# Last expert's tail, last chunk's products, slot lists and turned rows rearranged in a hybrid layer with expert-choice MoE

## Chip, core and metric

The kernel is one program on one core of one Trainium2 chip. The metric is the device time of an execution in microseconds (us). Engines are named as in the profile: PE (TensorE matmul), PEld (its weight load), DVE (VectorE), ACT (ScalarE), POOL (GpSimd), SP (the queue that issues most DMAs).

## What is computed

One layer over 1024 tokens of width 1024, 256 context tokens, then a last RMSNorm. The first half (norm, projection, three mixers, merge) is not touched by the change. What follows it is:

```python
h2 = modulate(x, norm2_g, sh2, sc2)
x = x + g2 * expert_choice_ffn(h2, w_router, w_gate, w_up, w_down)
return rmsnorm(x, final_norm_g)

def expert_choice_ffn(...):            # 16 experts, each takes its 128 best tokens
    gates, idx = lax.top_k(affinity.T, cap)
    xg = h[idx]
    a, u = xg @ w_gate[e], xg @ w_up[e]            # 1024 -> 2816
    y = (silu(a) * u) @ w_down[e] * gates          # 2816 -> 1024
    return zeros.at[idx].add(y)
```

All data is fp32. A product is made of three matmuls on values split into a high part that TensorE takes at full speed (fp32r) and the rest.

## The kernel before

`moe` streams the weights of the 16 experts through the core. An expert's 2816 hidden columns are cut into six **chunks** (0 to 5): five of 512 columns and a last one of 256. A weight piece is loaded in two **halves**, and a half is the unit of everything: `halves` lists them in the order of the products, for each expert chunk by chunk gate (2 halves), up (2), down of the chunk before (2), and after the last chunk its own down (2). That makes 36 halves for an expert, 576 in all; the halves of the last chunk hold 128x1024 elements, all others 128x2048.

- `load(j)` issues the DMA of half j from SP into a ring of twelve 1 MB tiles (`RING`). SP takes its DMAs in order, so one that waits holds up all behind it.
- `split(j)` makes the two parts of half j in one of four `whl` buffers: ACT copies the high part (line 67), DVE subtracts it for the rest (line 68).
- `products(j)` runs the matmuls through `mm3` (lines 72 to 74): 12 pairs of gate or up for a half, into PSUM tiles `w_gate` and `w_up`, or `y` for down.
- `silu` (ACT, line 1203) and `gated` (DVE, line 1206) make the chunk's activations, `turn` (line 1212) transposes them on PE two halves later, and line 67/68 split them into `aT` for the down products.
- The next expert's tokens are prepared inside the current one, at chunk 2: `choose_hot` makes a one-hot matrix (DVE, line 1099), `choose_rows` multiplies it with `tv` (eight matmuls, line 1109) which gives the token numbers and gates, and POOL gathers the rows (line 1114). At chunk 4 `turned` transposes the rows on PE (line 1134), for the first half of the columns before the second gate half, for the other before the second up half, and applies the modulation: ACT writes the high part (line 1138) and again the fp32 value (line 1142), DVE subtracts (line 1143).
- `scaled` (DVE, line 1222) and `scatter` (POOL, line 1226) add an expert's result to the DRAM tensor `xacc`, six halves into the next expert.

PE, ACT and DVE are under a manual schedule there: they run in the order in which the Python code emits them. The loop emits for half j what stands in `before[j]`, its products, then `split(j + 4)` and `load(j + 15)`, then what stands in `after[j]`. So a late instruction on DVE or ACT holds up what is behind it there. Ahead of that stage (and for POOL and SP in it) a scheduler places instructions by their dependencies.

`final` runs when the last expert has ended: it loads all of `xacc` (line 1319), adds the last expert's rows by matmuls with a one-hot matrix (lines 1335, 1337), squares and sums each of eight 128-row tiles (ACT, line 1339), makes the reciprocal root (`rstd`), scales (DVE line 1349, or ACT and POOL) and stores eight tiles from SP (line 1350).

## Time and profile before

| what | us |
|---|---|
| median of three runs | 2874.66 (2870.95 to 2875.48) |
| the profiled execution | 2874.45, its span 2872.7 |
| first product of the expert stage starts | 1310.67 |
| last product of the last expert starts | 2841.33 |
| PE, DVE, ACT busy in 100 us of the stage (1800 to 1900) | 99.60, 89.89, 77.65 |

The span is what the profile covers; 1.75 us of the profiled execution lie outside it. The busy time of PE is that of pipelined matmuls: a busy PE is not PE at its peak. An engine's share is an average over the stage; what a change is worth is read from what the next instruction waits for.

### The profile page before, as it was taken

The page shows a single profiled execution, that of the slowest core. Times are in us where ns is not written, and L with a number is a line of the kernel's source. Part 1 is how long each engine was busy: PE and PEld are TensorE (multiplying, and loading weights), DVE is VectorE, ACT ScalarE, POOL GpSimd, SP SyncE. Part 2 cuts the span into 40 slices and gives each one's busy share as a digit, 9 for nine tenths or more (in the row PEclk, how much of TensorE's full clock was granted, in tenths as well). Part 3 has the DMA queues.
Part 4 walks back from the last instruction along what each step waited for, and adds up shares of the span by engine and source line. Part 5 has one row for each costly group of instructions (what it writes and reads, how often), then busy time and mean ns, then how long its engine had stood idle before and what let it go on. Part 6 is the DMA issues. An engine that isn't in the chain of part 4 may idle for free.

```text
span 2872.7 us, 36082 instructions
## 1 busy us (share of the span) xinstructions
PE 2773.3 (97%) x13607; PEld 2299.9 (80%) x13607; DVE 2036.5 (71%) x2412; ACT 1685.7 (59%) x2005; POOL 290.2 (10%) x452
## 2 busy tenths in 40 slices
PE   7999999999999989987999999999999999999997
PEld 3888888888788878866888888888888888888885
DVE  4423231234578873478889988998899889988998
ACT  5412121212068981345777777777777777777775
POOL 1111000000144420000000000000000000000000
PEclk9999999999999999998999999999999999999998
DMA  8433231224977847558999999999999999999995
GB/s 251 176 125 143 81 136 55 78 98 137 298 202 216 208 161 252 163 169 308 340 369 378 375 376 369 379 376 372 369 381 379 370 369 380 379 373 366 375 381 197
DMA packets 344303, 783.54 MB, mean 273 GB/s; under 512 B 17288, under 2 KB 61008, under 8 KB 344000
## 3 DMA queue, kind: packets, MB, share of 16 engines
q1 hardware_dynamic: 321920, 705.09, 69.5%
q0 software_dynamic: 21968, 75.99, 7.7%
q8 instruction: 107, 1.75, 0.2%
q14 instruction: 68, 0.56, 0.1%
q10 hardware_dynamic: 240, 0.16, 0.0%
HBM read 710.37 MB, written 70.80 MB: 272 GB/s over the span
## 4 chain that ended last, share of the span: by engine, by line
PE 46%; ACT 3%; DMA 2%; DVE 2%; issue 1%; DVEq 0%
PE y L74 5%; PE y L72 5%; PE y L73 5%; PE w_gate L74 5%; PE w_gate L72 5%; PE w_gate L73 5%; PE w_up L72 5%; PE w_up L74 5%; PE w_up L73 5%; DMA wraw<-in_w_up 2%; PE tp L1212 2%; ACT whl L67 1%; DVE whl L68 1%; ACT xT L1138 1%; ACT a L1142 1%
## 5 line engine op out<-in xcount | busy, mean ns | idle before, releaser
L68 DVE TENSOR_TENSOR whl<-wraw,whl 128x2048 fp32r<-128x2048 f32 (+1 forms) x656 | 1292.2, 1996 | 211.9 <-ACT whl L67 209.6
L67 ACT CAST whl<-wraw 128x2048 fp32r<-128x2048 f32 (+1 forms) x660 | 1091.2, 1671 | 413.7 <-PE y L74 125.0
L73 PE MATMUL mm<-hT,whl 128*128 128x512 f32 x768 | 301.1, 392 | 1.6 <-DVE hT L278 1.6
L72 PE MATMUL mm<-hT,whl 128*128 128x512 f32 x768 | 300.4, 392 | 1.5 <-ACT hT L272 1.5
L74 PE MATMUL mm<-hT,whl 128*128 128x512 f32 x768 | 301.0, 392 | 0.0
L74 PE MATMUL w_gate<-whl,xT 128*128 128x512 f32 (+1 forms) x768 | 286.9, 374 | 2.8 <-DVE xT L1143 2.8
L72 PE MATMUL w_gate<-whl,xT 128*128 128x512 f32 (+1 forms) x768 | 289.6, 377 | 0.0
L72 PE MATMUL w_up<-whl,xT 128*128 128x512 f32 (+1 forms) x768 | 288.3, 375 | 0.0
L73 PE MATMUL w_gate<-whl,xT 128*128 128x512 f32 (+1 forms) x768 | 286.4, 373 | 0.0
L74 PE MATMUL w_up<-whl,xT 128*128 128x512 f32 (+1 forms) x768 | 285.8, 372 | 0.0
L73 PE MATMUL w_up<-whl,xT 128*128 128x512 f32 (+1 forms) x768 | 285.4, 372 | 0.0
L72 PE MATMUL y<-whl,aT 128*128 128x512 f32 x704 | 282.0, 401 | 0.0
L74 PE MATMUL y<-whl,aT 128*128 128x512 f32 x704 | 275.3, 391 | 0.0
L73 PE MATMUL y<-whl,aT 128*128 128x512 f32 x704 | 274.9, 391 | 0.0
L72 PEld LDWEIGHTS mm<-hT,whl 128*128 128x128 f32 x768 | 144.9, 189 | 37.5 <-ACT sg L534 5.2
L73 PEld LDWEIGHTS mm<-hT,whl 128*128 128x128 f32 x768 | 145.5, 189 | 31.9 <-DVE hT L278 2.0
L74 PEld LDWEIGHTS mm<-hT,whl 128*128 128x128 f32 x768 | 145.3, 189 | 29.9
L74 PEld LDWEIGHTS w_gate<-whl,xT 128*128 128x128 f32 x768 | 145.3, 189 | 29.2 <-DVE xT L1143 3.5
L73 PEld LDWEIGHTS w_gate<-whl,xT 128*128 128x128 f32 x768 | 145.5, 189 | 25.0
L74 PEld LDWEIGHTS w_up<-whl,xT 128*128 128x128 f32 x768 | 144.7, 188 | 25.6
L72 PEld LDWEIGHTS w_gate<-whl,xT 128*128 128x128 f32 x768 | 145.4, 189 | 24.7
L1226 POOL DMA_INDIRECT xacc<-yo,tok x15 | 50.5, 3364 | 1132.7 <-DVE yo L1222 1132.7
(355 smaller groups left out, 4423.3 us busy)
## 6 DMA issues: line engine op xcount, KB each, us to landing
wraw<-in_w_gate SPq DMA_DIRECT2D x160, 1024.0 KB, 11.1
wraw<-in_w_up SPq DMA_DIRECT2D x160, 1024.0 KB, 8.8
wraw<-in_w_down SPq DMA_DIRECT2D x160, 1024.0 KB, 11.8
wraw<-in_w_in SPq DMA_DIRECT2D x28, 1024.0 KB, 5.5
wraw<-in_ada_w SPq DMA_DIRECT2D x24, 1024.0 KB, 6.8
wraw<-in_w_gate SPq DMA_DIRECT2D x32, 512.0 KB, 12.0
wraw<-in_w_up SPq DMA_DIRECT2D x32, 512.0 KB, 9.3
wraw<-in_w_down SPq DMA_DIRECT2D x32, 512.0 KB, 5.9
```

The costliest lines, as they stand in the source:

```text
L67: self.nc.scalar.copy(hi, src)
L68: (eng or self.nc.vector).tensor_sub(lo, src, f(hi))
L72: mm(out, lh, rh, start=start, stop=False, **kw)
L73: mm(out, lh, rl, start=False, stop=False, **kw)
L74: mm(out, ll, rh, start=False, stop=stop, **kw)
L1138: nc.scalar.activation(ex.xT[:, 0, kk], tp[:, cs], AF.Identity, bias=B, scale=A)
L1142: nc.scalar.activation(h32[:, cs], tp[:, cs], AF.Identity, bias=B, scale=A)
L1212: nc.tensor.transpose(tp[:, 128 * k:128 * k + 128], ex.ready[:, 128 * k:128 * k + 128], self.ident)
L1226: nc.gpsimd.indirect_dma_start(out=self.xacc[:, :], out_offset=bass.IndirectOffsetOnAxis(ap=ex.tok, axis=0), in_=ex.yo, in_offset=None, co ...
```

## The change

1. **Final norm beside the last expert.** `final` is gone. In the last expert's loop, five tiles of the ring are taken out for good: one for the final gain and a scratch, four for `xacc` (1 MB each). The table `late` gives the half, counted from the end (H = 544), at which each step is emitted: the rows that the last expert adds to are gathered (H-29), eight squares on ACT (H-22 to H-12), two `rstd` (H-18, H-5), eight scalings on DVE with their stores from SP (H-14 to H-3). After the loop the last expert's 128 rows are finished apart: `scaled`, plus the gathered rows, square, `rstd`, scale, and one indirect store over the rows of `out`. In the last two halves the products of the first 512 columns of `y` all come before those of the others.
2. **Last chunk's gate and up in one product.** A half of kind `both` holds 256 columns of gate and 256 of up (two DMAs of 512 KB), and a product of 512 columns takes the place of two of 256. An expert has 34 halves. `silu` and `gated` of that chunk both follow its second half.
3. **Lists turned later.** `choose_list` multiplies the other way round (the one-hot matrix moves, `tv` is the weight) into 4x128, DVE copies that, and three halves later `choose_rows` transposes it on PE and goes on as before.
4. **Rows turned in fp32 first.** `turned` writes the fp32 values by ACT, then one ACT copy and one DVE subtraction of 512 columns. Its second half is emitted six halves after chunk 4's first gate half (ahead of the first `both` half), no longer three.
5. A Silu on ACT is written ahead of the first loads, and the ring's twelve tiles come from pools of 3, 1, 5 and 3 (before: 3, 5, 1, 3).

```diff
-    def rstd(self, ss, pool, tag):
+    def rstd(self, ss, pool, tag, eps=None):
...
+        if eps is not None:
+            nc.scalar.activation(s, ss, AF.Sqrt, scale=1.0 / D, bias=eps)
         nc.vector.tensor_scalar(v, ss, 1.0 / D, EPS, op0=ALU.mult, op1=ALU.add)
-        nc.scalar.sqrt(s, v)
+        if eps is None:
+            nc.scalar.sqrt(s, v)
...
-            ring_pool("wraw3", 5)
-            ring_pool("wraw4", NR - 8 - 3)
+            ring_pool("wraw3", 1)
+            ring_pool("wraw4", NR - 7)
...
+            def choose_list(ex):
...
-                    nc.tensor.matmul(tp[:, :4], hot[:, c], self.tv[:, c, e], start=c == 0, stop=c == CB - 1)
+                    nc.tensor.matmul(tp[:4, :128], self.tv[:, c, e], hot[:, c], start=c == 0, stop=c == CB - 1)
+                ex.list = sp.tile([4, 128], F32, name="list", bufs=1)
+                nc.vector.tensor_copy(ex.list, tp[:4, :128])
+
+            def choose_rows(ex, held=None):
+
+                tp = pst.tile([128, 512], F32, name="tp")
+                nc.tensor.transpose(tp[:, :4], ex.list, self.ident[:4, :4])
...
-                    nc.scalar.activation(ex.xT[:, 0, kk], tp[:, cs], AF.Identity, bias=B, scale=A)
...
-                nc.vector.tensor_sub(ex.xT[:, 1, 4 * b:4 * b + 4], h32.rearrange("p (k t) -> p k t", t=128),
-                                     f(ex.xT[:, 0, 4 * b:4 * b + 4]))
+                    nc.scalar.activation(h32[:, cs], tp[:, cs], AF.Identity,
+                                         bias=shift[:, kk:kk + 1], scale=scale[:, kk:kk + 1])
+                ks = slice(4 * b, 4 * b + 4)
+                self.split(ex.xT[:, 0, ks], ex.xT[:, 1, ks], h32.rearrange("p (k t) -> p k t", t=128))
...
-                    todo = [("w_gate", c), ("w_up", c)] + [("w_down", c - 1)] * (c > 0) + [("w_down", c)] * (c == last)
+                    todo = [("both", c)] if c == last else [("w_gate", c), ("w_up", c)]
+                    todo += [("w_down", c - 1)] * (c > 0) + [("w_down", c)] * (c == last)
...
+            def finish_load(i):
+                t = fin[i] = ring_tile(keep=True)
+                if i == 0:
+                    g = io["final_norm_g"]
+                    nc.sync.dma_start(t[:, :D], bass.AP(tensor=g.tensor, offset=g.offset, ap=[[0, 128], [1, D]]))
+                else:
+                    nc.sync.dma_start(t.rearrange("p (s d) -> p s d", s=2),
+                                      self.xacc[256 * (i - 1):256 * i].rearrange("(s p) d -> p s d", s=2))
...
+            def finish_square(i):
...
+                nc.scalar.activation(fin[0][:, D:], fin_row(i), AF.Square,
+                                     accum_out=fin["ss", i // 4][:, i % 4:i % 4 + 1])
...
+            def finish_store(i):
+                x = fin_row(i)
+                nc.vector.scalar_tensor_tensor(x, x, fin["r", i // 4][:, i % 4:i % 4 + 1], fin[0][:, :D],
+                                               op0=ALU.mult, op1=ALU.mult)
+                nc.sync.dma_start(io["out"][128 * i:128 * i + 128], x)
...
+            late = {H - 29: [lambda ex: finish_rows(ex)]}
+            for i, lag in enumerate((22, 21, 20, 19, 17, 15, 14, 12)):
+                late.setdefault(H - lag, []).append(lambda ex, i=i: finish_square(i))
+            late.setdefault(H - 18, []).append(lambda ex: finish_rstd(0))
+            late.setdefault(H - 5, []).append(lambda ex: finish_rstd(1))
+            for i, lag in enumerate((14, 12, 8, 7, 4, 4, 3, 3)):
+                late.setdefault(H - lag, []).append(lambda ex, i=i: finish_store(i))
+
+            def stream(j):
+
+                if j < FIN:
+                    load(j)
+                elif j < FIN + 5:
+                    finish_load(j - FIN)
+                else:
+                    load(j - 5)
...
+                if j == H - 2:
+                    return
+                if j == H - 1:
+
+                    for b in range(2):
+                        bs = slice(512 * b, 512 * b + 512)
+                        for kk in range(n // 128):
...
+            nc.scalar.activation(self.cs[:, 0, 0:1], self.ident[:, 0:1], AF.Silu)
             AHEAD = 4
...
+                if s == 1 and w == "both":
+                    silu(ex, ex.h[w][:, :n])
+                    gated(ex, ex.h[w][:, n:2 * n])
+
+                    put(after, j + 1, ("first", lambda ex=ex, c=c, n=n: turn(ex, c, n)))
...
-                        put(before, j + 3, lambda nx=nxt: choose_rows(nx))
+                        put(before, j + 3, lambda nx=nxt: choose_list(nx))
+                        put(before, j + 6, lambda nx=nxt: choose_rows(nx))
                     if c == 4:
                         put(before, j + 1, lambda nx=nxt: turned(nx, 0))
-                        put(before, j + 3, lambda nx=nxt: turned(nx, 1))
+                        put(before, j + 6, lambda nx=nxt: turned(nx, 1))
...
-            for b in range(2):
-                scaled(ex, b)
-            order.close()
-            rawst.close()
-            self.final(psg, ex.yo, ex.gate)
-
-    def final(self, psg, y, gate):
...
+            ss = sp.tile([128, 4], F32, name="ss")
             for b in range(2):
                 cs = slice(512 * b, 512 * b + 512)
+                scaled(ex, b)
+                nc.vector.tensor_add(ex.yo[:, cs], ex.yo[:, cs], ex.xg[:, cs])
+                nc.scalar.activation(fin[0][:, D:][:, cs], ex.yo[:, cs], AF.Square, accum_out=ss[:, b:b + 1])
+            nc.vector.tensor_add(ss[:, 2:3], ss[:, 0:1], ss[:, 1:2])
+            r = self.rstd(ss[:, 2:3], sp, "rl", fin["eps"])
+            nc.vector.scalar_tensor_tensor(ex.yo, ex.yo, r, fin[0][:, :D], op0=ALU.mult, op1=ALU.mult)
+
+            nc.gpsimd.indirect_dma_start(
+                out=io["out"][:, :], out_offset=bass.IndirectOffsetOnAxis(ap=ex.tok, axis=0),
+                in_=ex.yo, in_offset=None)
```

How the order on the engines moves is told at three places. The first is DVE at chunk 4 of an expert that has a next one (`xT` are the next expert's rows, `a` the gated activations, `aT` their split, `whl` the weights), before:

```order
L68 TENSOR_TENSOR whl<-wraw,whl 128x2048 x2
L1143 TENSOR_TENSOR xT<-a,xT 128x512
L68 TENSOR_TENSOR whl<-wraw,whl 128x2048
L68 TENSOR_TENSOR whl<-wraw,whl 128x1024
L1143 TENSOR_TENSOR xT<-a,xT 128x512
L1206 TENSOR_TENSOR a<-a,w_up 128x512
L68 TENSOR_TENSOR whl<-wraw,whl 128x1024 x2
L68 TENSOR_TENSOR aT<-tp,aT 128x512
```

and after:

```order
L68 TENSOR_TENSOR xT<-a,xT 128x512
L68 TENSOR_TENSOR whl<-wraw,whl 128x2048 x2
L1289 TENSOR_TENSOR a<-a,w_up 128x512
L68 TENSOR_TENSOR whl<-wraw,whl 128x2048 x2
L68 TENSOR_TENSOR aT<-tp,aT 128x512
L68 TENSOR_TENSOR whl<-wraw,whl 128x2048
L68 TENSOR_TENSOR xT<-a,xT 128x512
L68 TENSOR_TENSOR whl<-wraw,whl 128x1024
L1289 TENSOR_TENSOR a<-a,w_gate 128x256
```

The second `xT` stood right ahead of chunk 4's gated product and now stands behind that chunk's `aT`.

The second is DVE at the very end, after (`rfr` is the result of `rstd` for row tiles 4 to 7, `rl` belongs to that of the last expert's rows, `wraw` is a tile of rows of `xacc`):

```order
L1191 SCALAR_TENSOR_TENSOR wraw<-wraw,rfr 128x1024 x4
L1305 SCALAR_TENSOR_TENSOR yo<-y_21647,gate,g2b 128x512
L1390 TENSOR_TENSOR yo<-yo,xg 128x512
L1305 SCALAR_TENSOR_TENSOR yo<-y_21648,gate,g2b 128x512
L1390 TENSOR_TENSOR yo<-yo,xg 128x512
L1392 TENSOR_TENSOR ss<-ss 128x1
L112 TENSOR_SCALAR rlv<-ss 128x1
L115 RECIPROCAL rlr<-rls 128x1
L116 TENSOR_TENSOR rls<-rlr 128x1
L117 TENSOR_TENSOR rls<-rls,rlv 128x1
L118 TENSOR_SCALAR rls<-rls 128x1
L119 TENSOR_TENSOR rlr<-rlr,rls 128x1
```

Four scalings of 1024 columns stand ahead of the last expert's own result; before, 16 additions and the eight tiles' norms stood behind it. The last scaling (line 1394) and POOL's store follow.

The third is ACT in the gate projection of the first half of the program, long before the experts (`sg` a sigmoid), before:

```order
L534 ACTIVATE sg<-mm 128x512 x16
L599 ACT_TABLE_LOAD
L599 ACTIVATE ss<-ident 128x1
```

and after:

```order
L537 ACTIVATE sg<-mm 128x512 x12
L1324 ACT_TABLE_LOAD
L1324 ACTIVATE cs<-ident 128x1
L537 ACT_TABLE_LOAD
L537 ACTIVATE sg<-mm 128x512 x4
L602 ACT_TABLE_LOAD
L602 ACTIVATE ss<-ident 128x1
```

The Silu that is written at the head of the expert stage (line 1324) was placed there by the scheduler, between sigmoids; a table load ahead of the first expert's Silu is still in ACT's order (`L1285 ACT_TABLE_LOAD`).

## Rows read from the trace of the kernel before

**Rows 1.** Windows: us, then busy PE, PEld, DVE, ACT, POOL (count), PEclk, DMA, GB/s

```profile
1800.00:1900.00 100.00, 99.60 (x480) 83.00 (x479) 89.89 (x60) 77.65 (x67) 4.17 (x2) 1.00 1.02 374
```

**Rows 2.** Timeline, PE, chunks 4 and 5: start, us, instruction [idle before <-releaser]

```profile
1869.35 0.39 PE L72 MATMUL y<-whl,aT 128*128 128x512 f32 x1
...
1871.84 0.39 PE L74 MATMUL y<-whl,aT 128*128 128x512 f32 x1
1872.63 0.63 PE L1212 MATMUL tp<-ident,a 128*128 128x128 f32 x4 [0.40 <-DVE a L1206]
...
1875.86 0.28 PE L72 MATMUL w_gate<-whl,xT 128*128 128x256 f32 x1
...
1881.61 0.40 PE L72 MATMUL y<-whl,aT 128*128 128x512 f32 x1
```

**Rows 3.** Timeline of ACT and DVE around the same place

```profile
1860.44 1.91 ACT L67 CAST whl<-wraw 128x2048 fp32r<-128x2048 f32 x1 [0.81 <-PE w_gate L74]
...
1862.38 2.29 DVE L68 TENSOR_TENSOR whl<-wraw,whl 128x2048 fp32r<-128x2048 f32 x1 [0.43 <-ACT whl L67]
...
1871.80 0.68 DVE L1206 TENSOR_TENSOR a<-a,w_up 128x512 f32<-128x512 f32 x1
```

**Rows 4.** Timeline of PE: the row numbers' eight matmuls, and attention's with 128 columns

```profile
1926.51 0.95 PE L1109 MATMUL tp<-tv,xg 128*128 128x4 f32 x8
1927.31 0.49 PE L72 MATMUL w_up<-whl,xT 128*128 128x512 f32 x1
...
829.27 0.71 PE L667 MATMUL av<-pt,V 128*128 128x128 f32 x4
829.81 0.28 PE L712 MATMUL S<-kst,ql 128*128 128x256 f32 x1
```

**Rows 5.** Timeline of ACT and PE where the first expert begins

```profile
1310.16 0.46 ACT L1138 ACTIVATE xT<-tp,mod 128x128 fp32r<-128x128 f32 x1 [26.79 <-PE tp L1134]
...
1314.66 0.79 PE L74 MATMUL w_gate<-whl,xT 128*128 128x512 f32 x1 [2.77 <-DVE xT L1143]
...
1324.69 1.28 ACT L1203 ACT_TABLE_LOAD   x1
1325.99 0.60 ACT L1203 ACTIVATE a<-w_gate 128x512 f32<-128x512 f32 x1
```

**Rows 6.** Timeline of PE, DVE, ACT and SP's queue behind the last product

```profile
2841.33 0.39 PE L74 MATMUL y<-whl,aT 128*128 128x512 f32 x1
2841.08 1.43 DVE L1222 SCALAR_TENSOR_TENSOR yo<-y,gate,g2b 128x512 f32<-128x512 f32 x2 [2.73 <-PE y L74]
...
2847.13 1.06 ACT L1339 ACTIVATE o<-xt 128x1024 f32<-128x1024 f32 x1
...
2849.65 0.17 DVE L112 RECIPROCAL rfr<-rfs 128x2 f32<-128x2 f32 x1
...
2852.09 1.28 DVE L1349 SCALAR_TENSOR_TENSOR o<-xt,rfr,fg 128x1024 f32<-128x1024 f32 x1
2853.39 15.83 SPq L1350 DMA_DIRECT2D out<-o  x8
```

**Rows 7.** Timeline of POOL and windows late in the last expert, columns as in rows 1

```profile
2771.14 3.39 POOL L1226 DMA_INDIRECT xacc<-yo,tok  x1 [75.51 <-DVE yo L1222]
...
2805.00:2810.00 5.00, 5.00 (x26) 4.12 (x25) 4.65 (x4) 4.12 (x3) 0.00 (x0) 1.00 1.04 404
...
2815.00:2820.00 5.00, 5.00 (x24) 4.14 (x23) 4.15 (x2) 3.84 (x4) 0.00 (x0) 1.00 0.00 0
```

**Rows 8.** Waits of SP's queue; DMA issues: count, KB each, median us to landing

```profile
SPq L1165 <- DVE whl L68: 793.2, 369, 5.1
...
out<-o SPq DMA_DIRECT2D x8, 512.0 KB, 2.8
...
xg<-h2d,first POOLq DMA_INDIRECT x1, 5.5
...
xacc<-yo,tok POOLq DMA_INDIRECT x15, 11.2
```

More of the change, by code (lines that the diff above doesn't have):

```diff
@@ L1084, in moe, with ring_tile @@
             g2b = self.bcast(sp, self.modd[:, 3 * D:4 * D], "g2b")
-            cnt = [0]
-            class Ring:
-                def tile(_, *a, **k):
-                    cnt[0] += 1
-                    return raws[(cnt[0] - 1) % NR].tile(*a, **k)
-            ring = Ring()
+            slots = list(range(NR))
+            def ring_tile(keep=False):
+                i = slots.pop(0)
+                if not keep:
+                    slots.append(i)
+                return raws[i].tile([128, 2048], F32, name="wraw")
             chunks = [(512 * c, min(512, FF - 512 * c)) for c in range((FF + 511) // 512)]
@@ L1248, in moe @@
             for j in range(9, NR):
-                load(j)
+                stream(j)
             split(0, 1024)
@@ L1252, in moe @@
             for b in range(2):
-                turned(ex, b, nc.vector)
+                turned(ex, b)
             split(2, 1024)
@@ L1256, in moe @@
             for j in range(NR, NR + AHEAD - 1):
-                load(j)
+                stream(j)
             before, after = {}, {}
@@ L1268, in moe @@
                 if s == 1 and w == "w_up":
-                    gated(ex, n)
-                    if c == last:
-                        split(j + AHEAD - 1)
-                        put(after, j + 1, ("first", lambda ex=ex, c=c, n=n: turn(ex, c, n)))
-                    else:
-                        put(before, j + 2, lambda ex=ex, c=c, n=n: turn(ex, c, n))
+                    gated(ex, ex.h[w])
+                    put(before, j + 2, lambda ex=ex, c=c, n=n: turn(ex, c, n))
+                if s == 1 and w == "both":
+                    silu(ex, ex.h[w][:, :n])
+                    gated(ex, ex.h[w][:, n:2 * n])
+                    put(after, j + 1, ("first", lambda ex=ex, c=c, n=n: turn(ex, c, n)))
                 todo = after.pop(j, [])
@@ L1279, in moe @@
                         fn()
-                if (w, c, s) != ("w_up", last, 0):
-                    split(j + AHEAD)
-                load(j + AHEAD + NR - 1)
+                split(j + AHEAD)
+                stream(j + AHEAD + NR - 1)
                 for kind, fn in todo:
@@ L1354, in _constants @@
+            order.close()
 def _constants():
```

105 lines of the change are left out of this document (42 added, 63 removed).

## Prediction

> **What bounds the kernel now.** Read first the busy time by stretch. In 100 us from the middle of the experts PE is busy 99.60, and the clock granted to it is 1.00 throughout [rows 1]; DVE is at 89.89, ACT at 77.65. DMA's share reads 1.02 at 374 GB/s, which looks like a bound and isn't: SP's loads wait for DVE's split to give a ring tile back [rows 8], so a transfer starts when a tile is free, not when the DMA engines are. Read next PE's timeline at an expert's last two chunks. Eleven steps from 1869.35 to 1871.84 give 0.2264 us for a product of 512 columns, 2.72 for the twelve of a half. Then stands the one regular hole: the transposes (L1212) start 0.79 after the matmul before them, where 0.23 is the pace, and what released them is DVE's gated product of chunk 4 [rows 2]. Read last the timeline of ACT and DVE: ACT's copy of a half takes 1.91 and waited 0.81 for PE to give the buffer back; DVE's subtraction takes 2.29 and waited 0.43 for ACT [rows 3]. So both engines follow PE, with little to spare. Outside the stage there are two places: its first product stalls for its tokens [rows 5], and behind the last product there are 31.1 us (2841.33 + 0.23 = 2841.56 to the span's end, 2872.7) in which PE does next to nothing [rows 6].
>
> The sum goes against the profiled execution, 2874.45, which is 0.21 below the median of the runs, so a difference needs no conversion.
>
> **One product for the last chunk.** 48 matmuls of 256 columns take 1881.61 - 1875.86 = 5.75 [rows 2]. 24 of 512 at 0.2264 take 5.43. The bytes and the DMA issues stay the same in number, and two copies of 2048 replace four of 1024 on ACT and DVE. PE is the bound, so the 0.32 counts in each of 16 experts: **-5.1**.
>
> **The second turned half moves behind chunk 4's activations.** Before, its subtraction and the wait for ACT ahead of it stand in DVE's queue right in front of the gated product that PE waits for. After, that product has only splits ahead of it. The hole of 0.79 - 0.23 = 0.56 goes in the 15 experts that prepare a next one: **-8.5**. What could be late next is the same product for another reason: its SiLU and the splits of 1.91 and 2.29 around it [rows 3]. I count it as ending some 0.1 to 0.2 ahead of its need, by laying the rows' durations in the new order, so part of the hole may stay: 0 to -8.5. The subtraction's new place is ahead of the first joint half's split; there DVE has one gated product of half the width in place of a full one. The moved transposes on PE are the same in number.
>
> Eight ACT writes of 0.46 for a half of the rows become four and a copy of about 0.60 (the 512-wide SiLU's duration) [rows 5]. ACT waits for PE in the stretch, so this only takes work from an engine with spare: 0.
>
> **The list.** Before, eight matmuls with 4 columns take 1927.31 - 1926.51 = 0.80, and the next product's first step is 0.1 longer: 0.9 [rows 4]. After, eight matmuls move 128 columns. No row shows these operands. The nearest is attention's 128-column matmul at (829.81 - 829.27) / 4 = 0.135 [rows 4]; half of a 256-column pace of 0.12 [rows 2] would be 0.06. That is 0.5 to 1.1, and the transpose three halves later adds about 0.2 with its bubble: 0.7 to 1.3. I take 1.0, nearer to the row with this shape: 0.1 x 16 = **+1.6** (-3 to +6). The gather is issued three halves, 8.2 us, later. It lands in 5.5 to 11.2 [rows 8] and its rows are wanted seven halves, 19 us, after the new place, so POOL's gather stays hidden. The DVE copy of 4 rows is about 0.2, as the small operations of [rows 6], and hides in PE's product.
>
> **Where the first expert begins.** ACT's four writes alternate with DVE's from 1310.16 to PE's third matmul at 1314.66, 4.5 us [rows 5]. After: four writes in a row, at most 4 x 0.46, a copy of 0.60 and a subtraction of 0.68 [rows 3], 3.1: -1.4. Against it the first list gets a copy and a transpose on the path, 0.2 + 0.13 and two hand-overs, some 0.7. Sum **-0.7** (-1.4 to +1.5, since PE's first products there run at twice the usual time, 0.79 against 0.39 [rows 2, 5], and more of them may). The new Silu ahead of the loads sits among ACT's sigmoids long before, where ACT waits for PE: 0. The table load ahead of the first expert's SiLU stays.
>
> **The last expert's added work.** ACT gets eight squares of 1.06 [rows 6] and two table loads of 1.28 [rows 5], 11.1 us between the 22nd and the 5th half from the end, 17 x 2.72 = 46 us. Its spare there is 22.35% [rows 1], 10.3. A half may be late: with four buffers ACT and DVE have three halves, 8.2, for 1.91 + 2.29, so 4.0 of slack, less than the four squares and two loads that come close together (4 x 1.06 + 2 x 1.28 = 6.8, against 1.8 of spare in three halves: 5.0 late). DVE gets four scalings of 1.28 ahead of its last splits [rows 6], 5.1, in 38 us with 10% spare, 3.9: absorbed by the slack. So **+2** (0 to +6).
>
> [...] The row shows a table load of 1.28 with the SiLU starting 1.30 after the load's start, nothing between [rows 5]. [...]
>
> **The end.** DVE's last split ended 3.2 before the last product, and four scalings of 1.28 now follow it: free at about 1.5 behind the last product (0.9 to 1.9). Then twice the scaled result (0.72) and an addition (0.68), 2.8; a square of 512 with its sum, 0.8; eight small operations at 0.2, 1.6; a scaling of 1.28 [rows 6]; 1.5 + 2.8 + 0.8 + 1.6 + 1.3 = 8.0. SP's last four stores, about 2 us apart (15.83 for eight [rows 6]), run beside this. POOL's indirect store of 128 rows is not in the trace: its bounds are a plain store's 2.8 and the adding scatter's 11.2, and I take 5.5, the gather of the same rows on a quiet machine [rows 8]. The span ended 0.7 behind the last store (2853.39 + 15.83 + 2.8 = 2872.0). So 8.0 + 5.5 + 0.7 = 14.2 in place of 31.1: **-16.9** (-20 to -11).
>
> [...]
>
> **Sum.** -5.1 - 8.5 + 1.6 - 0.7 + 2 - 16.9 = -27.6: 2874.45 - 27.6 = **2847**.
>
> **The rivals.** The hole stays (0.20). If the SiLU or a split makes chunk 4's product late again, the 8.5 are not had: 2855. For it: DVE waits 0.43 for ACT at each split [rows 3], and the margin is a tenth of a microsecond. Against it: what the trace shows in front of it is what moves away.
>
> The last expert starves (0.17). Before, the weights are all in 26 us before the last product: 404 GB/s at 2805, 0 at 2815 [rows 7]. After, 4.7 MB of `xacc` and gain, 0.5 of gathered rows and six stores of 0.5 must fit in: 8.3 MB at 374 GB/s are 22 us, in those 26. The ring falls from twelve tiles to seven, and the reload of `xacc` waits for a scatter issued at 2771.14 that lands 11.2 later [rows 7, 8], with the weights behind it in SP's order. A load is then issued six halves, 16 us, ahead of its split. PE would wait 2 to 9 us; at 5: 2852.
>
> A new wait in every expert (0.05), the one that ends on the slower side. The last chunk's SiLU and gated product both follow the second joint half, and the turn comes one half later. ACT and DVE have about 1.8 us of margin there by the order. If a copy and a subtraction, 1.91 + 2.29 [rows 3], stand ahead of them, PE stalls 2.4 in 16 experts: +38, 2885. It ends slower once they are over 3.5 later than counted: 1.8 of margin, and 27.6 / 16 = 1.7 a time to use up the gain. Against it: ACT waits for PE in most halves.
>
> It doesn't do what it says (0.04): the early Silu is among the sigmoids and adds two table loads there, 2.6, if ACT turns out to be the bound in that stage: 2850.
>
> **How the numbers follow.** The forecast has 0.54; its own bounds and the first two rivals, singly or together (2860), make the range 2837 to 2861. Its lower end is the cheap list (-4.6), the store in 2.8 (-2.7) and the last expert's work at 0 (-2); its upper end is the hole and the starved loads together. About 0.2% (5.7 us) is what a measurement can tell from no change; only both rivals with the list and the store at their upper ends come within it: 0.03. Slower is the new wait: 0.05. Faster 0.92.
>
> **What would show it.** In the profile after: 24 matmuls of 512 columns for the last chunk in 5.4; L1212's counterpart at chunk 4 within 0.3 of the matmul ahead; the list's eight matmuls near 0.8; PE's wait at the first expert near 3; in the last 60 us PE idle 2 in all, with waits for ACT's splits and not for weights; 14 us from the last product to the end, half of it POOL's store. An expert's period should fall by 0.8 (0.32 + 0.56 - 0.1). If PE waits at the joint halves' turn, or the last expert shows waits for DMA, the forecast is wrong there.

## The result and the profile after

The changed kernel takes 2843.3 us (median of four, 2840.24 to 2845.05) against 2872.8 for the kernel before in the same session: a ratio of 0.9897, interval 0.9885 to 0.9909, so 29.5 us or 1% faster. The forecast was 2847, range 2837 to 2861. The profiled execution took 2844.3, its span 2842.5, and the account below is made against the profiled execution of before, 30.15 us longer.

The middle of the stage, a window of the changed kernel with the columns of [rows 1]:

```profile
1800.00:1900.00 100.00, 100.00 (x463) 82.21 (x462) 90.92 (x60) 75.92 (x60) 4.17 (x2) 1.00 1.03 380
```

PE has no idle time left there. The timeline of PE in the same two chunks as [rows 2], changed kernel (L1295 are the transposes of chunk 4, L1145 those of the second half of the next rows; the 24 products of gate and up in one start at 1962.78, and the last row is the first product behind them):

```profile
1958.98 0.40 PE L74 MATMUL y<-whl,aT 128*128 128x512 f32 x1
1959.22 0.60 PE L1295 MATMUL tp<-ident,a 128*128 128x128 f32 x4
...
1962.42 0.60 PE L1145 MATMUL tp<-ident,xg 128*128 128x128 f32 x4
1962.78 0.47 PE L72 MATMUL w_gate<-whl,xT 128*128 128x512 f32 x1
...
1968.35 0.39 PE L72 MATMUL y<-whl,aT 128*128 128x512 f32 x1
```

The transposes follow 0.24 behind the matmul ahead of them, where it was 0.79 [rows 2]. The joint product runs from 1962.78 to the next at 1968.35, 5.57 for what took 5.75. In the last expert, where no transposes of next rows stand right ahead of it, it takes 5.44. One expert after the other starts 94.45 us apart (94.43 to 94.48, 14 of them) where it was 95.40.

The end of the program, changed kernel, timelines of PE, DVE and POOL (columns as in [rows 6]):

```profile
2829.17 0.39 PE L74 MATMUL y<-whl,aT 128*128 128x512 f32 x1
...
2825.77 4.86 DVE L1191 SCALAR_TENSOR_TENSOR wraw<-wraw,rfr 128x1024 f32<-128x1024 f32 x4
2830.55 0.74 DVE L1305 SCALAR_TENSOR_TENSOR yo<-y,gate,g2b 128x512 f32<-128x512 f32 x1
...
2834.20 0.16 DVE L1392 TENSOR_TENSOR ss<-ss 128x1 f32<-128x1 f32 x1 [0.79 <-ACT wraw L1391]
...
2835.68 1.28 DVE L1394 SCALAR_TENSOR_TENSOR yo<-yo,rlr,wraw 128x1024 f32<-128x1024 f32 x1
...
2837.25 0.97 POOL L1396 DMA_INDIRECT out<-yo,tok  x1 [68.62 <-DVE yo L1394]
```

and the DMA issues of its two kinds of store (columns as in [rows 8]):

```profile
out<-wraw SPq DMA_DIRECT2D x8, 512.0 KB, 2.7
...
out<-yo,tok POOLq DMA_INDIRECT x1, 3.3
```

From the last product (2829.17 + 0.23 = 2829.40) to the end of the span are 13.1 us, where there were 31.1.

There is also a new loss, in the last expert, which lasts 96.8 us from its first product (2732.36) to the last where it lasted 92.6 before. The timelines of ACT, DVE and PE there, changed kernel:

```profile
2780.85 1.89 ACT L67 CAST whl<-wraw 128x2048 fp32r<-128x2048 f32 x1
2782.76 1.28 ACT L111 ACT_TABLE_LOAD   x1
2784.06 0.30 ACT L111 ACTIVATE rfs<-ss,eps 128x4 f32<-128x4 f32 x1
2784.26 1.89 ACT L67 CAST whl<-wraw 128x2048 fp32r<-128x2048 f32 x1
2786.17 1.28 ACT L1285 ACT_TABLE_LOAD   x1
2787.46 0.60 ACT L1285 ACTIVATE a<-w_gate 128x512 f32<-128x512 f32 x1
...
2790.92 2.29 DVE L68 TENSOR_TENSOR whl<-wraw,whl 128x2048 fp32r<-128x2048 f32 x1 [2.44 <-ACT whl L67]
2793.13 0.68 DVE L1289 TENSOR_TENSOR a<-a,w_up 128x512 f32<-128x512 f32 x1
...
2793.87 0.65 PE L1295 MATMUL tp<-ident,a 128*128 128x128 f32 x4 [2.67 <-DVE a L1289]
...
2795.30 0.63 PE L73 MATMUL y<-whl,aT 128*128 128x512 f32 x1
2795.73 0.63 PE L74 MATMUL y<-whl,aT 128*128 128x512 f32 x1
```

and a window of it, columns as in [rows 1]:

```profile
2770.00:2790.00 20.00, 20.00 (x92) 16.55 (x91) 16.22 (x15) 19.94 (x22) 0.00 (x0) 1.00 1.04 399
```

ACT is busy 19.94 of 20 us, DVE only 16.22: DVE's split ahead of the gated product waits 2.44 for ACT's copy, and PE waits 2.67 for the gated product. Behind that wait eight products come at 0.43 in place of 0.23: the granted clock reads 0.66 from 2795 to 2800, and 0.50 from 2795.30 to 2798.20. Together that is 4.3 us.

### The profile page after: what moved, and what is told of

Same layout as the page of the kernel before. It is cut to its first block, busy times and chain, and to the rows that moved or that the text cites. A ratio compares the mean times of both kernels' runs of the same rounds, so it can differ in the third digit from the quotient of the medians.

```text
span 2842.5 us, 35023 instructions
## 1 busy us (share of the span) xinstructions
PE 2755.7 (97%) x13207; PEld 2270.1 (80%) x13207; DVE 2026.7 (71%) x2370; ACT 1662.3 (58%) x1887; POOL 287.1 (10%) x452
## 4 chain that ended last, share of the span: by engine, by line
PE 89%; DVE 3%; ACT 3%; issue 2%; DMA 1%; POOL 1%; POOLq 0%; SPq 0%; DVEq 0%; ACTq 0%
PE mm L73 10%; PE mm L72 10%; PE mm L74 10%; PE w_gate L72 6%; PE w_gate L74 6%; PE w_gate L73 6%; PE y L74 5%; PE y L72 5%; PE y L73 5%; PE w_up L72 5%; PE w_up L74 5%; PE w_up L73 5%; PE tp L1295 1%; PE av L670 1%; PE S L715 1%
## 5 line engine op out<-in xcount | busy, mean ns | idle before, releaser
L72 PE MATMUL w_gate<-whl,xT 128*128 128x512 f32 x768 | 306.3, 399 | 1.4 <-ACT xT L67 1.4
L74 PE MATMUL w_gate<-whl,xT 128*128 128x512 f32 x768 | 300.5, 391 | 0.0
L73 PE MATMUL w_gate<-whl,xT 128*128 128x512 f32 x768 | 300.1, 391 | 0.0
L72 PE MATMUL w_up<-whl,xT 128*128 128x512 f32 x640 | 250.1, 391 | 0.0
L73 PE MATMUL w_up<-whl,xT 128*128 128x512 f32 x640 | 249.2, 389 | 0.0
L74 PE MATMUL w_up<-whl,xT 128*128 128x512 f32 x640 | 249.2, 389 | 0.0
L74 PEld LDWEIGHTS y<-whl,aT 128*128 128x128 f32 x704 | 132.6, 188 | 28.7
L73 PEld LDWEIGHTS y<-whl,aT 128*128 128x128 f32 x704 | 132.8, 189 | 25.5
```

The costliest lines, as they stand in the source:

```text
L72: mm(out, lh, rh, start=start, stop=False, **kw)
L73: mm(out, lh, rl, start=False, stop=False, **kw)
L74: mm(out, ll, rh, start=False, stop=stop, **kw)
```

## Experiments

The period of an expert (start of one to start of the next, in the middle of the stage) is the finest measure here, since the part ahead of the experts differs between executions: in the profiles of kernels that are the same up to there, the first product of the first expert starts anywhere from 1309.3 to 1312.7, and the changed kernel's own profile is the latest of them. Times are medians; ratios stand against the kernel before in the same session. A difference to the changed kernel compares medians of two sessions, and the changed kernel's four runs lie 4.8 apart, so the stretches of the trace decide what an edit did.

**The second turned half's place, in the kernel before.**

```diff
-                        put(before, j + 3, lambda nx=nxt: turned(nx, 1))
+                        put(before, j + 6, lambda nx=nxt: turned(nx, 1))
```

> The kernel before with one number changed: the second turned half is emitted six halves after chunk 4's first gate half in place of three. Theory (its place in DVE's queue makes the hole): PE's 0.40 us waits at chunk 4's transposes go in 15 experts, an expert's period falls from 95.40 by 0.56 to 94.84, the time falls by 8.5 us against the kernel before. Rival (the eight ACT writes and not the place make the hole): in the new place the same work delays something else, PE keeps a wait of 0.3 us or more an expert, and the time changes by less than 3 us.

Measured: 2890.83, ratio 1.0065 (1.0048 to 1.0082), so slower by 18.3; period 96.65. Waits of PE by releaser (us in total, times, longest):

```profile
PE y L73 <- DVE whl L68: 24.6, 15, 1.6
```

The wait at chunk 4's transposes is gone, as the theory said, and another of 1.64 stands in its place in each of 15 experts, in the expert's last down products. DVE and ACT in front of it:

```profile
1976.21 1.05 ACT L67 CAST whl<-wraw 128x1024 fp32r<-128x1024 f32 x1 [1.66 <-PE y L74]
1977.16 0.45 ACT L1138 ACTIVATE xT<-tp,mod 128x128 fp32r<-128x128 f32 x1
...
1979.91 3.73 ACT L67 CAST whl<-wraw 128x2048 fp32r<-128x2048 f32 x2
...
1980.08 0.69 DVE L1143 TENSOR_TENSOR xT<-a,xT 128x512 fp32r<-128x512 f32 x1 [1.57 <-ACT a L1142]
1981.88 4.50 DVE L68 TENSOR_TENSOR whl<-wraw,whl 128x2048 fp32r<-128x2048 f32 x2 [1.10 <-ACT whl L67]
```

The last chunk's four short halves keep PE 1.44 each, and in their time the down products' full halves are to be split, 2.29 each on DVE. In the new place ACT's eight writes (2.75 us, 1977.16 to 1979.91) stand in front of these splits. So the move by itself is a loss of 1.25 an expert. The theory fell. Of the rival the mechanism came true (the same work delays something else, with a wait of over 0.3), and its size, under 3 us, did not.

**The same place undone in the changed kernel.**

```diff
-                        put(before, j + 6, lambda nx=nxt: turned(nx, 1))
+                        put(before, j + 3, lambda nx=nxt: turned(nx, 1))
```

> The changed kernel with the second turned half emitted three halves after chunk 4's first gate half again. Theory (place): the hole is back, an expert's period rises from 94.45 to about 95.0, the time rises by 8.5 us against the changed kernel, some 2852. Rival (fp32 first, with three ACT instructions fewer, had closed it by itself): period 94.45, time unchanged within 2 us. Between the two, since ACT's part is 0.9 us shorter than in the kernel before, the hole may be partly closed: 0 to 8.5.

Measured: 2844.53, ratio 0.9905 (0.9889 to 0.9922); period 94.55. The rival holds: with the rest of the change in, the place is worth 0.1 an expert. What closed the hole had to be another part.

**fp32 first, alone in the kernel before.**

```diff
-                    nc.scalar.activation(ex.xT[:, 0, kk], tp[:, cs], AF.Identity, bias=B, scale=A)
                     if eng is not None:
+                        nc.scalar.activation(ex.xT[:, 0, kk], tp[:, cs], AF.Identity, bias=B, scale=A)
...
+                if eng is None:
+                    ks = slice(4 * b, 4 * b + 4)
+                    self.split(ex.xT[:, 0, ks], ex.xT[:, 1, ks], h32.rearrange("p (k t) -> p k t", t=128))
+                    return
```

> The kernel before with one part of the change: inside the expert loop `turned` writes the rows in fp32 by four ACT instructions and splits them by one copy and one subtraction; both halves keep their places and the first expert's form is as before. Theory formed from the two runs before this one (what held chunk 4's gated product was ACT's eight writes, on which DVE's subtraction ahead of it waited 0.80 us): PE's wait of 0.40 goes in 15 experts, the period falls from 95.40 to about 94.85, the time by 8 us against the kernel before. Rival (the joint gate and up product, or the list's later turn, closed the hole): the wait stays at 0.3 or more, the time within 2 us of before.

Measured: 2865.45, ratio 0.9971 (0.9962 to 0.9981), so 8.2 faster; period 94.82, 0.58 below the kernel before. In the middle experts PE waits for nothing; of the 16 waits at L1212's counterpart one is left, at the first expert:

```profile
PE tp L1216 <- DVE a L1210: 0.6, 1, 0.6
```

In the kernel before, DVE's subtraction of the second half stood right ahead of the gated product and waited for ACT, which had no idle moment between 1860.44 and 1872.10 (DVE's timeline and a window, columns as in [rows 1]; the third line is the same subtraction in this run):

```profile
1871.19 0.69 DVE L1143 TENSOR_TENSOR xT<-a,xT 128x512 fp32r<-128x512 f32 x1 [0.80 <-ACT a L1142]
...
1860.44:1872.10 11.66, 11.66 (x56) 9.46 (x54) 8.83 (x7) 11.66 (x21) 0.00 (x0) 1.00 0.90 306
...
1866.28 0.69 DVE L68 TENSOR_TENSOR xT<-a,xT 128x512 fp32r<-128x512 f32 x1
```

So the length of ACT's eight writes in that place is enough to make the hole: with shorter work in the same place it is gone. The move takes the same hole away, but opens a larger one. ACT needs 1.50 for four writes and 0.62 for the copy in the changed form, where the eight took 2.75.

**Both of the old form and the old place, in the changed kernel.** The four writes and the split become the eight writes again, and the place is three halves.

```diff
+                    nc.scalar.activation(ex.xT[:, 0, kk], tp[:, cs], AF.Identity, bias=Q, scale=P)
+                    nc.scalar.activation(h32[:, cs], tp[:, cs], AF.Identity, bias=Q, scale=P)
...
-                        put(before, j + 6, lambda nx=nxt: turned(nx, 1))
+                        put(before, j + 3, lambda nx=nxt: turned(nx, 1))
```

> The changed kernel with `turned` as before in both respects: eight ACT writes and one subtraction, second half three halves after chunk 4's first gate half. Theory (ACT's writes): PE waits 0.4 at chunk 4's transposes again, the period is 94.95 to 95.05 in place of 94.45, the time 8 us above the changed kernel, and the first expert's start is some 1 us later besides. Rival (the joint product or the list closed the hole): period 94.45 to 94.6, time within 3 us of the changed kernel.

Measured: 2861.72, ratio 0.996 (0.9946 to 0.9974), 18.4 above the changed kernel; period 95.85 to 95.97. The place is the predicted one, the size is not:

```profile
PE tp L1296 <- DVE a L1290: 23.0, 17, 2.7
```

The wait is 1.28 an expert, not 0.40. With the joint product the splits ahead of chunk 4's gated product are both of 2048 columns, where before the second was a short one. In the run with the place undone and four writes DVE takes 4.58 for this pair, before 3.43:

```profile
1857.65 4.58 DVE L68 TENSOR_TENSOR whl<-wraw,whl 128x2048 fp32r<-128x2048 f32 x2 [0.96 <-ACT whl L67]
1862.14 0.69 DVE L68 TENSOR_TENSOR xT<-a,xT 128x512 fp32r<-128x512 f32 x1
1862.74 0.68 DVE L1289 TENSOR_TENSOR a<-a,w_up 128x512 f32<-128x512 f32 x1
```

So at the old place the joint product needs the cheaper turned rows: with the old ones the period is 0.5 above that of the kernel before. No run has the old rows at the new place.

**Gate and up of the last chunk apart, in the changed kernel.**

```diff
-                    todo = [("both", c)] if c == last else [("w_gate", c), ("w_up", c)]
+                    todo = [("w_gate", c), ("w_up", c)]
...
```

The steps of `late` and the ring's switch are moved by two halves to keep their places.

> The changed kernel with the last chunk's gate and up apart again: four halves of 128x1024 with products of 256 columns, the last expert's steps kept at their places. Theory by the prediction (only PE's time changes): the period rises by 0.32 to 94.77, the time by 5 us. Rival, from the kernel before with the second turned half moved (there PE came to wait 1.64 us an expert for DVE's split in the last down products, because four short halves of 1.44 us ask for splits of 2.29): with ACT's work 0.9 us shorter a wait of about 0.7 is left, the period is some 95.5 and the time 15 us or more above the changed kernel.

Measured: 2888.1, ratio 1.0053 (1.0036 to 1.007), 45 above the changed kernel; period 97.44, 3.0 more. The theory by the prediction falls, and the rival has the place and direction right and the size too small, for which the edit has a part:

```profile
PE y L73 <- DVE whl L68: 13.6, 15, 0.9
...
PE tp L1295 <- DVE a L1289: 17.2, 18, 2.9
```

A wait of 0.9 stands at the down products in every expert that prepares a next one, and one of about 0.86 at the last chunk's transposes, in the last expert too, which has no rows to turn. The second wait comes from something else than the four short halves and the moved one. The kernel before emits one split of the last chunk late, behind that chunk's gated product (`split(j + AHEAD - 1)`). The change dropped this together with the short halves, and this run doesn't bring it back. DVE's timelines, first this run, then the kernel before with the second half moved:

```profile
1981.60 5.63 DVE L68 TENSOR_TENSOR whl<-wraw,whl 128x2048 fp32r<-128x2048 f32 x3 [1.11 <-ACT whl L67]
1987.14 0.41 DVE L1289 TENSOR_TENSOR a<-a,w_up 128x256 f32<-128x256 f32 x1
...
1986.29 0.42 DVE L1206 TENSOR_TENSOR a<-a,w_up 128x256 f32<-128x256 f32 x1
```

Three splits of 5.63 in all stand ahead of the gated product here, where there were two of 4.50 (1981.88, above). So the run shows that the moved half makes the down products wait where the short halves are kept, 0.9 here and 1.64 above. It doesn't show what the joint product alone is worth; no run has the short halves, the cheaper rows and the late split together.

**The list as before, in the changed kernel.**

```diff
-                    nc.tensor.matmul(tp[:4, :128], self.tv[:, c, e], hot[:, c], start=c == 0, stop=c == CB - 1)
+                    nc.tensor.matmul(tp[:, :4], hot[:, c], self.tv[:, c, e], start=c == 0, stop=c == CB - 1)
...
-                        put(before, j + 3, lambda nx=nxt: choose_list(nx))
-                        put(before, j + 6, lambda nx=nxt: choose_rows(nx))
+                        put(before, j + 3, lambda nx=nxt: (choose_list(nx), choose_rows(nx)))
```

> The changed kernel with the list made as before: the eight matmuls with 4 columns, and row numbers and gather straight behind them, no transpose three halves later. The prediction counted the new list 0.1 us dearer an expert (1.6 in all, -3 to +6). The two traces show 0.94 against 0.95 us an expert for all of it, so this run should stand within 1 us of the changed kernel, with an expert's period of 94.45 within 0.1. Rival (the list's move frees POOL, the gather or DVE where it counts): the period rises by 0.2 or more, the time by 3 us or more.

Measured: 2838.83, ratio 0.9882 (0.9866 to 0.9899), 4.5 below the changed kernel, where the theory allowed 1; the two intervals overlap. The period is 94.40, 0.05 less, 0.75 over 15 experts. In the profiles, 1.6 more is in the last expert, and not the list: PE waits there 2.69 at the same transposes, but the products behind the wait come at a granted clock of 1.00.

```profile
2788.30 0.66 PE L1292 MATMUL tp<-ident,a 128*128 128x128 f32 x4 [2.69 <-DVE a L1286]
```

The timeline above is PE's in the run with the old list, and so are these windows, with the columns of [rows 1]:

```profile
2785.00:2790.00 5.00, 2.31 (x13) 1.68 (x12) 4.64 (x3) 5.00 (x6) 0.00 (x0) 1.00 1.03 396
2790.00:2795.00 5.00, 5.00 (x24) 4.13 (x23) 5.00 (x5) 3.94 (x5) 0.00 (x0) 1.00 1.10 351
```

The first expert starts at 1308.0, below all other profiles. That isn't the list either: from the start of the one-hot matrix on DVE to the row numbers it took 2.77 here (1295.95 to 1298.72), as in the kernel before (1300.14 to 1302.91), and 2.66 in the changed kernel (1300.57 to 1303.23). The earlier start lies ahead of the list. In the changed kernel the list's eight matmuls read, in PE's timeline:

```profile
1918.76 0.66 PE L1113 MATMUL tp<-xg,tv 128*4 128x128 f32 x8
1919.25 0.45 PE L72 MATMUL w_up<-whl,xT 128*128 128x512 f32 x1
```

They take 0.49 (1918.76 to 1919.25) where it took 0.80 [rows 4], and the transpose and what it delays take the difference back. Profiles with the new list and nothing else changed in the middle experts have periods of 94.42 to 94.46, this run and the last one below, both with the old list, 94.40 and 94.44. So the list's part of the change gains nothing, and a cost is not clear of that spread.

**The last expert without the two table loads.** The first root is a plain scaled copy, so the scale factors of row tiles 0 to 3 are not roots.

```diff
-    def rstd(self, ss, pool, tag, eps=None):
+    def rstd(self, ss, pool, tag, eps=None, root=AF.Sqrt):
...
-            nc.scalar.activation(s, ss, AF.Sqrt, scale=1.0 / D, bias=eps)
+            nc.scalar.activation(s, ss, root, scale=1.0 / D, bias=eps)
...
-                fin["r", g] = self.rstd(fin["ss", g], sp, "rf", fin["eps"])
+                fin["r", g] = self.rstd(fin["ss", g], sp, "rf", fin["eps"], AF.Sqrt if g else AF.Identity)
```

> The changed kernel with the first square root of the last expert (for row tiles 0 to 3) done as a plain scaled copy on ACT: the scale factors of these tiles are then wrong, and the two table loads in the middle of the last expert (1.28 each, one for the root, one back to SiLU) are not there. Theory (ACT has more work than time from 2770 to 2798): PE's wait of 2.67 us at 2793.87 falls to 0.2 or less, PE's half-clock stretch behind it (eight steps of 0.43, 1.6 us more) goes with it, time 4.2 us lower. Rival (the loads of weights come late there since the ring has seven tiles): the wait stays, time unchanged within 1 us.

Measured: 2837.85, ratio 0.9881 (0.9865 to 0.9898), 5.5 below the changed kernel. The last expert lasts 92.6 in place of 96.8, 4.2 less as the theory said, and PE waits at none of its transposes:

```profile
2788.34 0.66 PE L1295 MATMUL tp<-ident,a 128*128 128x128 f32 x4
```

Weights that come late are ruled out: the ring of seven tiles is the same here.

**The last expert's ACT work spread.**

```diff
-            for i, lag in enumerate((22, 21, 20, 19, 17, 15, 14, 12)):
+            for i, lag in enumerate((22, 20, 18, 16, 12, 10, 9, 8)):
...
-            late.setdefault(H - 18, []).append(lambda ex: finish_rstd(0))
+            late.setdefault(H - 14, []).append(lambda ex: finish_rstd(0))
...
-            for i, lag in enumerate((14, 12, 8, 7, 4, 4, 3, 3)):
+            for i, lag in enumerate((12, 10, 8, 7, 4, 4, 3, 3)):
```

> The changed kernel with the last expert's ACT work spread: squares at 22, 20, 18, 16, 12, 10, 9, 8 halves before the end (22, 21, 20, 19, 17, 15, 14, 12 in the changed kernel), the first root at 14 in place of 18, the first two scalings at 12 and 10 in place of 14 and 12. Nothing is left out. Theory (ACT's clustered work): the lateness of ACT stays under its 4.0 us of slack, PE's wait of 2.67 and its half-clock stretch go, time 4.2 us lower, about 2839. Rival (late weights): the wait stays where it is. A third outcome: a wait of about 1 us in the last 10 halves, where DVE's scalings and ACT's squares now come together, time 2 to 3 us lower.

Measured: 2839.71, ratio 0.9888 (0.9872 to 0.9905), 3.6 below the changed kernel; the last expert lasts 94.3, 2.5 less. It is the third outcome: the wait at chunk 3's transposes goes, and one of 1.79 comes at chunk 4's, where a scaling of 1.28 now stands in DVE's queue right ahead of the gated product, and the split ahead of both waited 0.68 for ACT.

```profile
2805.52 1.28 DVE L1191 SCALAR_TENSOR_TENSOR wraw<-wraw,rfr 128x1024 f32<-128x1024 f32 x1
2806.71 0.68 DVE L1289 TENSOR_TENSOR a<-a,w_up 128x512 f32<-128x512 f32 x1
...
2807.45 0.66 PE L1295 MATMUL tp<-ident,a 128*128 128x128 f32 x4 [1.79 <-DVE a L1289]
```

**Squares and gains on POOL.**

```diff
+                nc.gpsimd.tensor_mul(sq, fin_row(i), fin_row(i))
+                n = D // 2
+                while n > 32:
+                    nc.gpsimd.tensor_add(sq[:, :n], sq[:, :n], sq[:, n:2 * n])
+                    n //= 2
...
+                if i in (5, 7):
+                    nc.scalar.activation(x, x, AF.Identity, scale=r)
+                    nc.gpsimd.tensor_mul(x, x, fin[0][:, :D])
```

> A version meant to be better than both. The changed kernel with the squares of row tiles 4 to 7 on POOL (a product, five halving additions, one small DVE sum), the first root at 16 halves before the end in place of 18, and of the last four scalings the second and the fourth done by ACT (scale) and POOL (gain) while DVE does the other two. Nothing is left out. If ACT's 11 us of added work were the cause of PE's 2.67 us wait and the half-clock stretch, both go (4.2 us), as in the run without the table loads; DVE is free 2.4 us earlier behind the last product: together some 6 us below the changed kernel, 2837. Rival: POOL's work slows DVE's splits or comes late itself (four squares of some 7 us each in 38 us), a new wait of 1 us or more shows in the last expert, and the gain is under 4 us.

Measured: 2851.7, ratio 0.9926 (0.991 to 0.9943), 8.4 above the changed kernel. The rival holds. Groups of instructions by form between 2774 and 2827 (busy us, mean ns), DVE and POOL of this kernel:

```profile
L68 DVE TENSOR_TENSOR whl<-wraw,whl 128x2048 fp32r<-128x2048 f32 x14 | 39.0, 2815 | 1.1 <-ACT whl L67 1.0
L1209 DVE SCALAR_TENSOR_TENSOR wraw<-wraw,rfr 128x1024 f32<-128x1024 f32 x4 | 7.6, 1894 | 0.0
...
L1190 POOL TENSOR_TENSOR yo<-wraw 128x1024 f32<-128x1024 f32 x4 | 13.3, 3333 | 8.8 <-DMA wraw<-xacc 8.6
```

DVE's split takes 2.82 in place of 2.29 and its scaling 1.89 in place of 1.28. PE waits 3.56, 2.98 and 1.56 in the last expert.

**The root on DVE, no table loads, nothing left out.**

```diff
...
+                nc.vector.tensor_scalar(v, fin["ss", g], 1.0 / D, EPS, op0=ALU.mult, op1=ALU.add)
+                nc.vector.tensor_scalar(s.bitcast(I32), v.bitcast(I32), 1, None, op0=ALU.arith_shift_right)
+                nc.vector.tensor_scalar(r.bitcast(I32), s.bitcast(I32), -1.0, 1597463007.0, op0=ALU.mult, op1=ALU.add)
+                for _ in range(3):
+                    nc.vector.scalar_tensor_tensor(s, r, -0.5, r, op0=ALU.mult, op1=ALU.mult)
+                    nc.vector.tensor_mul(s, s, v)
+                    nc.vector.scalar_tensor_tensor(r, s, 1.5, r, op0=ALU.add, op1=ALU.mult)
...
+                if i < 7:
...
+            finish_store(7)
             nc.vector.tensor_add(ss[:, 2:3], ss[:, 0:1], ss[:, 1:2])
```

> A second version meant to be better than both, without POOL. The changed kernel with the first reciprocal root of the last expert made on DVE alone (a shift, a subtraction and three Newton steps, 12 operations of 128x4 in place of six and an ACT root), so that the two table loads in the middle go and nothing is left out; and with the eighth tile's scaling put behind the last expert's additions, where DVE waited 0.79 us for ACT's square. Theory: PE's 2.67 us wait and its half-clock stretch go as without the table loads (4.2 us), DVE has 1.2 us more to do, inside its slack; the tail is 0.8 us shorter. Sum 5 us below the changed kernel, some 2838. Rival (DVE's 12 operations, in a row ahead of a split, take the place of ACT's lateness): a wait of 1 us or more stays at chunk 3's transposes and the time is 2841 or above.

Measured: 2835.9 (2835.06 to 2837.4), ratio 0.9868 (0.9851 to 0.9884): the lowest median of all, 7.4 below the changed kernel, whose interval begins where this one ends. The wait at chunk 3's transposes is 1.41, half of what it was, and the products behind it come 0.23 apart; the last expert lasts 93.9, 2.9 less. The tail is 12.7, 0.4 less.

```profile
2788.93 0.66 PE L1307 MATMUL tp<-ident,a 128*128 128x128 f32 x4 [1.41 <-DVE a L1301]
```

So the theory and its rival both hold in part, and the trace accounts for 3.3 of the 7.4; the first expert starts 3.2 earlier in this profile, in a part that the edit doesn't touch.

**The same with the root behind the gated product.** Root at 15, squares at 22, 20, 19, 17, 15, 14, 13, 12, first scaling at 13, and the old list.

```diff
-            late.setdefault(H - 18, []).append(lambda ex: finish_rstd(0))
+            late.setdefault(H - 15, []).append(lambda ex: finish_rstd(0))
...
```

> The version without the table loads, with the DVE root emitted 15 halves before the end in place of 18, so that it stands behind chunk 3's gated product in DVE's queue and not ahead of it, squares at 22, 20, 19, 17, 15, 14, 13, 12, the first scaling at 13 in place of 14, and the list made as before the change. Theory (what is left of the wait, 1.41 us at chunk 3's transposes, is DVE's 12 operations and ACT's lateness ahead of that product): the wait falls to 0.3 or less, the last expert lasts some 92.7 us; with the list's 0.05 an expert and 0.5 at the first expert the time is 2833 to 2834, 2 to 3 us below that version. Rival (the same operations are late at the next place, chunk 4's transposes): a wait of 0.5 or more shows there and the time stays within 1.5 us of it.

Measured: 2839.19, ratio 0.9891 (0.9874 to 0.9907), 3.3 above that version, with intervals that overlap. The wait at chunk 3 is gone and one of 2.05 stands at chunk 4's transposes, as the rival said; the last expert lasts 94.9, 1.0 longer.

```profile
2806.22 0.66 PE L1304 MATMUL tp<-ident,a 128*128 128x128 f32 x4 [2.05 <-DVE a L1298]
```

## Why the prediction was right, and where it was not

The time was 3.7 us under the forecast and inside the range, on the way of the forecast's likeliest case. By its steps:

- **What bounds the kernel**: right. PE is the bound, each saved PE step shows in the period, and no wait for weights appears, in the last expert either.
- **One product and the moved half, -13.6 in all**: the sum came near, and the mechanism did not hold. With the list the prediction had 0.32 + 0.56 - 0.1 = 0.78 an expert; the period fell by 0.95. The joint product is right: 5.44 where no turn stands ahead of it, 0.31 less than before. The hole of 0.56 went too, but the step that was to pay for it failed. The prediction credited the move of the second half and took its new place as free, and it put the shorter ACT work at nothing, because ACT waits for PE in the stretch. The wait that it read stands at 1860.44; from there to 1872.10, where the hole is made, ACT has no idle time. Alone, the move costs 1.25 and the shorter work gains 0.58. In one order of the edits the runs give three steps: fp32 first 95.40 to 94.82 (-0.58), the joint product and the list, with the place still at three, to 94.55 (-0.27), the place to 94.45 (-0.10).
- **Edits costed one by one**: this is what the prediction missed altogether. Of the three only the cheaper rows gain by themselves. The place alone loses 1.25, and the joint product and the list with the old rows at the old place lose 0.5. That the 8.5 came out was luck: another part of the change earned them.
- **The list, +1.6 (-3 to +6)**: inside its bounds, and no cost clear of the spread shows. The eight matmuls, 0.06 each, are cheaper than attention's row of 0.135 said, and the transpose takes that back.
- **The first expert, -0.7 (-1.4 to +1.5)**: too small, and outside its bounds. From the rows' first transposes to the first up product it took 13.3 before and 11.0 after. From ACT's first write to PE's third product are 3.2 (1310.53 to 1313.75), where 3.1 was worked out and 4.5 stood before. But the new list's copy and transpose, +0.7 in the sum, cost nothing there (2.66 against 2.77), and the sum did not have the clock: ten products come at a granted clock of 0.50 (1312.7 to 1317.2), some 0.43 each in place of 0.23, where fourteen did before (0.50 from 1314.7 to 1319.9): four fewer, some 0.8.
- **The last expert, +2 (0 to +6)**: the mechanism was right, ACT's squares and table loads come too close for its slack, and the size was 4.3, of which the run without the two loads gives 4.2 back. The prediction counted an excess of 1.0 over the slack of 4.0 and took 2; 2.67 was the wait, and 1.6 came from the clock behind it (0.50 for eight products), for which no term stood in the sum.
- **Starved loads** (a rival): didn't happen. In the last expert ACT's copies waited for PE alone and DVE's splits for ACT alone, and no wait for a DMA shows on either.
- **The new wait at the joint halves' turn** (the slower rival): didn't happen; PE waits at no transposes in the middle experts.
- **The end, -16.9**: 18.0 measured. DVE was free at 1.15 behind the last product (1.5 predicted), its chain ended 7.6 behind it (8.0), the indirect store landed in 3.3 and not 5.5, and 1.9 were left behind it and not 0.7. The gather that was taken as the nearest row was the wrong one. Nearer were plain stores of 512 KB on POOL's queue: three kinds of them (`vd`, `qd`, `kd`) landed in 2.9 to 3.2 in the kernel before.
- **The table load**: as its row was read, 1.28 and then the next instruction. In the last expert ACT's copy ahead of the load ends at 2782.74, the load starts at 2782.76 and the root at 2784.06, 1.30 later; behind the second load the SiLU starts after 1.29 (2786.17 to 2787.46).

Added up: 15 periods of -0.95 are -14.2, the first expert's start and what lies ahead of it -2.1, the last expert +4.2, the end -18.0, together -30.1. Against the forecast the middle experts gave 2.2 more than their terms (-5.1 - 8.5 + 1.6 = -12.0) and the last expert cost 2.2 more: these two errors cancel, by luck.

## What to carry to other kernels

When a step waits on a queue, look at what the instruction ahead of it was itself waiting for: shortening that work took the hole away by itself (0.58 an expert), moving the instruction opened a larger one elsewhere (a wait of 1.64). Where engines run in a hand-made order with small slack, price parts of a change in the combination in which they run: the moved half cost 1.25 us an expert in the kernel before and gains 0.10 in the changed one. Work added to a stage fits by its peak, not by its average (ACT was busy 19.94 of 20 us in the last expert, 75.92 of 100 in the middle): sum what falls within the slack's few halves, and allow for what may come behind a wait of PE in clock, 1.6 us behind one of 2.67 here and nothing behind one of 2.69.

## What the runs showed of the hardware

In the last expert of the run with squares and gains on POOL, some instructions of DVE and POOL took longer than the same forms in the changed kernel or the kernel before. From 2774 to 2827 DVE's split of 128x2048 took 2.82 in the mean, against 2.29 in the changed kernel (2774 to 2822), its scaling 1.89 against 1.28, and one 128x4 operation 1.75 against 0.17. A 128x1024 product on POOL took 3.33 in the mean, against 2.34 to 2.36 behind the last expert in the kernel before. DVE's gated product of 128x512 kept its 0.68, and so did its split of `aT`, 128x512 too. No run shows why these two were spared.

PE's clock behind a wait doesn't follow from the wait's length alone. After a wait of 2.67 us the changed kernel ran eight products 0.43 apart, at a granted clock of 0.50. After one of 2.69 in the run with the old list they came 0.23 apart at 1.00. After 2.93 in the run with the place undone the granted clock read 0.78 from 2790 to 2795 and 0.87 from 2795 to 2800. After waits of 1.41 (the root on DVE) and 2.05 (the root behind the gated product) the products came 0.23 apart.
